# Four-tile weight rings, two sets of element loads, and 1 KB for dynamic DMAs' descriptors, in a two-layer RWKV-7 and S5 trunk

## The chip, the cores and the metric

The kernel runs on one core of one Trainium2 chip. The core has a matrix engine (TensorE, PE in the profile; its weight loads are listed as PEld), a vector engine (DVE), a scalar engine (ACT), GpSimd (POOL) and a sync engine (SP) that here issues nearly all transfers. Every engine works through its own list of instructions in the order in which the program holds them, and an instruction that waits holds up all that stand behind it on that engine. The metric is the device time of one execution in microseconds (us), as a median of several runs.

## The reference, cut to what matters

A sequence of 1024 frames with 1024 channels, in float32, goes through two layers. Layer 0 mixes over time with RWKV-7 (a matrix-valued state per head), layer 1 with a diagonal state-space layer (S5) and a gated linear unit; each mixer is followed by a squared-ReLU MLP with 4096 hidden channels, and each of the four sub-layers ends in a LayerNorm of `alpha * x + f(x)`.

```python
r, k, v = xr @ wr, xk @ wk, xv @ wv            # xr, xk, ... : x mixed with the frame before
a = sigmoid(a0 + (xa @ a1) @ a2);  g = sigmoid(xg @ g1) @ g2
state = state * w_t + sa * b_t + v_t * k_t     # per head, frame after frame
...
h = layer_norm(DN_ALPHA * h + mix, ...)
h = layer_norm(DN_ALPHA * h + square(relu(h @ w1)) @ w2, ...)
```

## The kernel before, in words

**Number format and weights.** Each float32 product is made of three products of a narrower type: an operand is split into a rounded part (hi) and the rest (lo). A weight tile of 128 x 512 numbers (256 KB, 2 KB of each partition) goes through three rings of the pool `wp`: `wraw` holds it as loaded by SP (line 215; lines 322, 476, 1135 and 1182 use the same ring), ACT casts it to `whi` (line 191 in `split`, or 220, 224), and DVE subtracts to get `wlo` (line 192), or `wlo` is loaded as it was saved earlier (line 223). `whi` and `wlo` are then read by the matmuls of line 256. `wraw` has two tiles, `whi` and `wlo` three each. A ring's tile can be written again only when its last reader is done, so SP waits at line 215 for ACT and DVE, ACT at line 191 for PE.

**Stages.** `rwkv_proj(0)` and `rwkv_proj(1)` make the projections r, k, v, a, g and the decay for the two halves (512 frames each) and store them in DRAM (`s_r`, `s_k`, `s_v`, `s_a`, `s_g`, `s_sg`). `core` then runs eight units of 256 frames x 512 channels, four per half. For a unit, `elem(m)` runs twice (j = 0, 1; I call these its two halves): it loads `ldk`, `ldsg`, `lda`, `ldr` (line 589), scans the decay (line 622 on DVE, which overwrites `ldsg`), makes `E` (line 625, ACT), `kf` (631 ACT, 633 and 643 POOL), `kk` (607, 620) and from these `AR` (636, 637) and `KB` (641, 642). `amat` (line 672, 676), `invert` (708 to 742) and the serial `chain` (780 to 803) follow, then `gnorm`. `KB` has two tiles, and a unit's `KB` is released by `kbtrans` (line 686) of that unit, so the next unit's first `KB` waits for it. The four `ld` tensors have one tile each: a half's loads wait for the last readers of the half before. Of these, line 642 reads `ldsg` last.

`wo(0)`, LayerNorm 1 and the MLP of the first half start when units 0 to 3 are through; from there on the MLP's matmuls fill PE. The S5 tables and `s5`, `glu`, the second MLP (`blocks`, and `both`, which shares products between the two halves) follow. The last blocks run in two column halves with kept weights (`kept`: `wraw` loaded at line 1135, cast to the tile `kt1` by ACT at line 1139), and `last_norm` ends the program.

**What sets the order.** Instructions are put in order per engine when the program is built, from their priorities (`rank`; a smaller number goes first), their dependencies and the free tiles of the rings. The first half of `rwkv_proj(0)` has the smallest numbers, units have 3000 upwards, and the rest of the projections 100000. A change of a ring's depth therefore moves instructions on all engines, although the set of instructions stays what it was.

Of the kernel before, what the change touches and what calls it, by code (L numbers as in the profile page):

```python
# [8 lines left out]
F32 = mybir.dt.float32  # L9
# [12 lines left out]
KB2 = 2  # L22
# [34 lines left out]
RK = (6000, 3000, 1000, 2500, 2000, 7000, 2600)  # L57
PB = 3
STB = 3
EB = (1, 1, 1, 1, (), 1)  # L60
GNG = (0, 0)
XM0 = False
G1L = True
# [16 lines left out]
def trunk(ctx, tc, A):  # L80
    nc = tc.nc
# [1 line left out]

    cp = ctx.enter_context(tc.tile_pool(name="cp", bufs=1))
    dr = ctx.enter_context(tc.tile_pool(name="dr", bufs=1, space=DRAM))
    wp = ctx.enter_context(tc.tile_pool(name="wp", bufs=3))
    ap = ctx.enter_context(tc.tile_pool(name="ap", bufs=1))
    tp = ctx.enter_context(tc.tile_pool(name="tp", bufs=2))
    pd = ctx.enter_context(tc.tile_pool(name="pd", bufs=3, space=PSUM))
# [78 lines left out]
    def weave(op, share=1.0):  # L168

        if anchor[0] is not None or not woven:  # L170
            return
        due[0] += share
        anchor[0] = op
        while due[0] >= 1 and woven:
            due[0] -= 1
            with rank(woven[0][1]):
                if next(woven[0][0], None) is None:
                    woven.pop(0)
                else:
                    woven[0][1] = tc.cur_priority  # L180
        anchor[0] = None
# [8 lines left out]
    def split(src, hi, lo, e=None):  # L190
        S.copy(hi, src)  # L191
        op = (e or V).tensor_sub(lo, src, hi.bitcast(F32))  # L192
        if e is None or e is V:
            behind(op)
            weave(op, pace_[0])
# [8 lines left out]
    nw = [0]  # L204
# [3 lines left out]
    def wload(src, kt, n, key=None, halved=False):  # L208

        step = 512 // n  # L210
        out = []
        for k0 in range(0, kt, step):
            kept = low.get((key, k0)) if key else None
            raw = wp.tile([128, step, n], F32, tag="wraw", name="wraw", bufs=2)
            SP.dma_start(raw, src[:, k0 : k0 + step])
            hi = wp.tile([128, step, n], F32R, tag="whi", name="whi")
            lo = wp.tile([128, step, n], F32R, tag="wlo", name="wlo")
            nw[0] += 1
            if halved:
                S.mul(hi, raw, 0.5)  # L220
                weave(V.scalar_tensor_tensor(lo, raw, 0.5, hi.bitcast(F32), op0=ALU.mult, op1=ALU.subtract))
            elif kept is not None:
                SP.dma_start(lo.bitcast(F32).rearrange("p k n -> p (k n)"), kept)
                S.copy(hi, raw)
            else:
                split(raw, hi, lo, G if nw[0] % WLG[0] in WLG[1] and WLG[2] <= nw[0] < WLG[3] else V)
                if key and key[0] not in ("mw1", "mw2"):
                    low[key, k0] = dr.tile([128, 512], F32, name=f"low{len(low)}")
                    SP.dma_start(low[key, k0], lo.bitcast(F32).rearrange("p k n -> p (k n)"))
            out += [(hi[:, k], lo[:, k]) for k in range(step)]  # L230
        return out
# [23 lines left out]
    def mmb(p, w, x, **kw):  # L255
        bulk.append((PE.matmul(p, w, x, **kw).ins, x.shape[-1]))  # L256

    def mm3(p, whi, wlo, xh, xl, first, last):
        mmb(p, whi, xh, start=first, stop=False)
        mmb(p, whi, xl, start=False, stop=False)  # L260
        mmb(p, wlo, xh, start=False, stop=last)
# [37 lines left out]
    def psd():  # L299
        pool, tag = banks[0][nb[0] % len(banks[0])]  # L300
        nb[0] += 1
        return pool.tile([128, HT], F32, tag=tag, name="d")
# [13 lines left out]
    def rwkv_proj(H):  # L316
# [1 line left out]
        xs = []  # L318

        def wraw(nm, k0):  # L320
            w = wp.tile([128, 4, 128], F32, tag="wraw", name="wsc", bufs=2)
            SP.dma_start(w, A[nm][:, k0 : k0 + 4])
            return w

        first = []
        for k in range(KT):
            t = ap.tile([128, HT + 1], F32, tag="xs", name="xs", bufs=8)
# [123 lines left out]
        def store_out(out, n, e):  # L451
            (ST if out in STO else SP).dma_start(scr[out][n * 128 : (n + 1) * 128, t0 : t0 + HT], e)
# [19 lines left out]
        def gate(n):  # L472
            if n % 4 == 0:
                wg[0] = wload(A["g2a"][:, n // 4], 4, 128, f"g2a{n}")
                rawb = wp.tile([128, 512], F32, tag="wraw", name="w2raw", bufs=2)
                SP.dma_start(rawb, A["g2b"][:, n * 128 : n * 128 + 512])
                wg[1] = wp.tile([128, 512], F32R, tag="whi", name="w2st")
                S.copy(wg[1], rawb)
                V.tensor_sub(wg[1][64:128], rawb[64:128], wg[1][64:128].bitcast(F32))
            q = n % 4  # L480
            p = psd()
            mm3(p, wg[0][q][0], wg[0][q][1], gx[0], gx[1], True, False)
            mmb(p, wg[1][:, q * 128 : (q + 1) * 128], h2, start=False, stop=True)
            e = tp.tile([128, HT], F32, tag="ev", name="ev", bufs=EVB)
            S.copy(e, p)
            store_out("g", n, e)
# [41 lines left out]
        else:  # L528
            for n in range(KT):
                rates(n)  # L530
            for n in range(KT):
                gate(n)
# [11 lines left out]
        for cb in range(4):  # L544
            pp = [psd(), psd()]
            for k0 in range(0, KT, 2):
                w = wload(A["wv"][cb][:, k0 : k0 + 2], 2, 256, f"wv{cb}-{k0}")
                for kk in range(2):
                    k = k0 + kk
# [28 lines left out]
    def elem(m):  # L578
# [5 lines left out]
        for j in range(2):  # L584
            n0 = 4 * D.q + 2 * j
            ld = {}
            for nm in ("k", "sg", "a", "r"):
                t = kp.tile([128, 512], F32, tag="ld" + nm, name="ld" + nm, bufs=EB[3] if nm in EB[4] else 1)
                SP.dma_start(t.rearrange("p (i t) -> p i t", i=2),
# [13 lines left out]

            sq = kp.tile([128, HT], F32, tag="sq", name="sq", bufs=EB[0])
            kk = kp.tile([128, HT], F32, tag="kk", name="kk", bufs=EB[1])
            for i in range(2):
# [15 lines left out]
            V.tensor_tensor_scan(cs, cmask.rearrange("p c l -> p (c l)"), cs, 0.0, op0=ALU.mult, op1=ALU.add)  # L622
            E = kp.tile([128, 8, L + 1], F32, tag="E", name="E", bufs=EB[5])
            G.memset(E[:, :, 0:1], 1.0)
# [3 lines left out]

            kf = kp.tile([128, HT], F32, tag="kf", name="kf", bufs=EB[2])
            for i in range(2):  # L630
# [483 lines left out]
    def blocks(i, h, xo, qbuf):  # L1114

        nw = 512 // KB2
        qs = {}

        def up(b):
            qs[b] = []  # L1120
            pace_[0] = PACEU[i]
            for n in range(KB2):
                p = psd()
                dense(p, wload(A["mw1"][i, b * KB2 + n], KT, 128, ("mw1", i, b * KB2 + n)), xo)
                r = tp.tile([128, HT], F32, tag="ev", name="rl", bufs=EVB)
                S.activation(r, p, AF.Relu)  # L1126
                S.activation(r, r, AF.Square)
                qt = qbuf[:, n + KB2 * (b % 2)]
                split(r, qt[:, 0], qt[:, 1])
                qs[b].append((qt[:, 0], qt[:, 1]))  # L1130
            pace_[0] = 1.0

        def kept(src, part):
            raw = wp.tile([128, KB2, nw], F32, tag="wraw", name="wraw", bufs=2)
            SP.dma_start(raw, src)
            hi, lo = (jp.tile([128, HT], F32R, tag=t, name="k" + t, bufs=8).rearrange("p (k n) -> p k n", k=KB2)
                      for t in ("t1", "t2"))
            SP.dma_start(lo.bitcast(F32).rearrange("p k n -> p (k n)"), part)
            S.copy(hi, raw)
            return [(hi[:, k], lo[:, k]) for k in range(KB2)]  # L1140

        def down(b, first=False, cs=slice(0, HT), keep=None):
            for n2 in range(C // nw):
                if keep is None:
                    w = wload(A["mw2"][i, b, n2], KB2, nw, ("mw2", i, b, n2))
                else:
                    if (b, n2) not in keep:
                        keep[b, n2] = kept(A["mw2"][i, b, n2], low[("mw2", i, b, n2), 0])
                    w = keep[b, n2]
                for n in range(nw // 128):  # L1150
                    p = psd()[:, cs]
                    dense(p, [(x[:, n * 128 : (n + 1) * 128], y[:, n * 128 : (n + 1) * 128]) for x, y in w],
                          [(x[:, cs], y[:, cs]) for x, y in qs[b]])
                    z = h[n2 * (nw // 128) + n][:, cs]
                    if first:
                        weave(V.scalar_tensor_tensor(z, z, ALPHA, p, op0=ALU.mult, op1=ALU.add), PACED[i])
                    else:
                        weave(V.tensor_add(z, z, p), PACED[i])  # L1158

        return up, down  # L1160
# [12 lines left out]
    def both(i, hP, hQ, P, Q, tops, first):  # L1173

        nw = 512 // KB2
# [2 lines left out]
        qs = {}  # L1178

        def raw(pool, tag, f, k0):  # L1180
            t = pool.tile([128, 4, 128], F32, tag=tag, name="raw", bufs=2)
            SP.dma_start(t, A["mw1"][i, f][:, k0 : k0 + 4])
            return t

# [477 lines left out]
    with rank(99100):  # L1662
        for k in range(4):
            a = t1[k]
# [107 lines left out]
```

## Time and profile before

| | before |
|---|---|
| median of 3 runs | 2596.31 us (2596.01 to 2599.6) |
| the profiled execution's own time | 2585.47 us |
| its span | 2583.5 us |
| mean granted PE clock | 0.975 of full speed |
| ACT, DVE, POOL busy | 1210.5, 1794.0, 406.0 us |
| loads of `wraw`, all lines together | 256 KB each, median 2.7 to 4.2 us to landing |

A column of waits reads "who waited, for whom: us in total, times, longest". In the table of windows each stretch has the busy time of each engine, then the mean granted clock of PE (1.00 is full speed), the share of the DMA engines that was busy, and GB/s. The chain of work that ended last is given as start, length and what ran; a chain that passes through an instruction says that nothing earlier could have released what came after it.

### The profile page before, as it was taken

What the parts mean: (1) busy time and instruction counts of PE and PEld (TensorE: products, weight loads), DVE (VectorE), ACT (ScalarE), POOL (GpSimd) and SP (SyncE); (2) the same over time, 40 slices, a digit from 0 to 9 for tenths busy, and PEclk for the clock granted to TensorE, in tenths of its full rate; (3) what the DMA queues carried; (4) which work ended last, traced back from release to release, by engine and by line L of the source; (5) the groups of instructions that cost most, each with busy time, mean ns of one, the idle gap of its engine ahead of it and who ended that gap; (6) DMA issues with size and microseconds to landing.
All of it is one profiled execution on the core that took longest, in us unless ns stands there. A gap on an engine that the chain in (4) does not pass through costs nothing.

```text
span 2583.5 us, 43873 instructions
## 1 busy us (share of the span) xinstructions
PE 2466.0 (95%) x16684; PEld 2002.0 (77%) x16684; DVE 1794.0 (69%) x3443; ACT 1210.5 (47%) x2165; POOL 406.0 (16%) x336
## 2 busy tenths in 40 slices
PE   7989989989989999999999999999999999999997
PEld 5779767788767888777777878887887888888886
DVE  7477687577787776899886665676657555656555
ACT  7555575454454443345634444334565333343334
POOL 3110441331211102001000000100222111111111
PEclk9999989999899999999999999999999999999998
DMA  4765455664222324446565553244261111111233
GB/s 152 261 200 184 160 198 172 190 186 152 93 70 78 104 86 126 141 122 165 162 226 192 176 175 111 95 162 160 94 197 60 49 54 50 48 58 49 78 122 114
DMA packets 217682, 340.66 MB, mean 132 GB/s; under 512 B 21248, under 2 KB 81792, under 8 KB 217472
## 3 DMA queue, kind: packets, MB, share of 16 engines
q1 hardware_dynamic: 216320, 335.77, 40.9%
q8 instruction: 131, 2.15, 0.4%
q10 hardware_dynamic: 1152, 2.10, 0.2%
q14 instruction: 79, 0.65, 0.1%
HBM read 267.53 MB, written 70.25 MB: 131 GB/s over the span
## 4 chain that ended last, share of the span: by engine, by line
PE 69%; DVE 13%; DMA 9%; ACT 5%; issue 3%; SPq 1%; POOL 0%; ACTq 0%; DVEq 0%; POOLq 0%
PE d L256 51%; PE d L1195 10%; DVE wlo L192 2%; PE pA L672 1%; DMA wraw<-in_mw_dram 1%; ACT whi L191 1%; DMA yl<-s_y 1%; DVE hA L1158 1%; DMA pre<-in_mw_dram 1%; DMA ldsg<-s_sg 1%; DMA s_y<-yg 1%; PE pR L780 1%; DMA lda<-s_a 1%; DVE oAl L192 1%; PE pq L934 1%
## 5 line engine op out<-in xcount | busy, mean ns | idle before, releaser
L191 ACT CAST whi<-wraw 128x512 fp32r<-128x512 f32 x424 | 261.6, 619 | 487.1 <-PE d L256 249.8
L192 DVE TENSOR_TENSOR wlo<-wraw,whi 128x512 fp32r<-128x512 f32 x424 | 317.4, 750 | 201.1 <-ACT whi L191 197.2
L256 PE MATMUL d<-qbuf,whi 128*128 128x512 f32 x1152 | 365.2, 399 | 9.8 <-ACT rl L1126 4.7
L256 PE MATMUL d<-oAh,whi 128*128 128x512 f32 (+1 forms) x752 | 303.2, 409 | 13.1 <-ACT ev L493 5.5
L256 PE MATMUL d<-oAl,whi 128*128 128x512 f32 (+1 forms) x752 | 302.1, 403 | 7.7 <-DVE oAl L942 4.4
L256 PE MATMUL d<-oAh,wlo 128*128 128x512 f32 (+1 forms) x752 | 301.2, 404 | 3.5 <-DMA wlo<-low 1.9
L256 PEld LDWEIGHTS d<-qbuf,whi 128*128 128x128 f32 x1152 | 212.2, 189 | 63.1 <-DVE hA L1158 7.8
L256 PE MATMUL d<-qbuf,wlo 128*128 128x512 f32 x576 | 225.5, 394 | 0.0
L256 PE MATMUL d<-oBh,whi 128*128 128x512 f32 x496 | 195.9, 395 | 0.4 <-DVE hA L1158 0.4
L256 PE MATMUL d<-oBh,wlo 128*128 128x512 f32 x496 | 195.8, 395 | 0.0
L256 PE MATMUL d<-oBl,whi 128*128 128x512 f32 x496 | 193.7, 391 | 0.0
L256 PEld LDWEIGHTS d<-oAh,whi 128*128 128x128 f32 (+1 forms) x752 | 143.1, 192 | 48.0 <-ACT ev L493 7.8
L256 PEld LDWEIGHTS d<-oAl,whi 128*128 128x128 f32 (+1 forms) x752 | 144.4, 193 | 38.7 <-DVE oAl L942 4.8
L256 PEld LDWEIGHTS d<-oAh,wlo 128*128 128x128 f32 (+1 forms) x752 | 144.3, 193 | 36.2 <-DVE wlo L192 2.7
L256 PE MATMUL d<-ql,whi 128*128 128x512 f32 x416 | 163.1, 392 | 0.0
L256 PE MATMUL d<-qh,whi 128*128 128x512 f32 x416 | 162.0, 389 | 0.0
L256 PE MATMUL d<-qh,wlo 128*128 128x512 f32 x416 | 158.0, 394 | 0.0
L256 PEld LDWEIGHTS d<-qbuf,wlo 128*128 128x128 f32 x576 | 108.9, 189 | 24.4 <-issue 0.5
L1158 DVE TENSOR_TENSOR hA<-hA,d 128x512 f32<-128x512 f32 x136 | 92.0, 683 | 28.8 <-PE d L256 27.7
L1158 DVE TENSOR_TENSOR hB<-hB,d 128x512 f32<-128x512 f32 (+1 forms) x160 | 97.6, 631 | 20.1 <-PE d L256 18.9
L256 PEld LDWEIGHTS d<-oBh,wlo 128*128 128x128 f32 x496 | 93.2, 188 | 21.9 <-issue 0.8
L256 PEld LDWEIGHTS d<-oBh,whi 128*128 128x128 f32 x496 | 93.3, 188 | 21.5 <-issue 2.0
(495 smaller groups left out, 5268.6 us busy)
## 6 DMA issues: line engine op xcount, KB each, us to landing
wraw<-in_mw_dram SPq DMA_DIRECT2D x356, 256.0 KB, 2.7
wlo<-low SPq DMA_DIRECT2D x92, 256.0 KB, 2.9
wraw<-in_glu_dram SPq DMA_DIRECT2D x64, 256.0 KB, 2.7
low<-wlo SPq DMA_DIRECT2D x52, 256.0 KB, 2.6
raw<-in_mw_dram SPq DMA_DIRECT2D x52, 256.0 KB, 2.7
wraw<-in_wk_dram SPq DMA_DIRECT2D x32, 256.0 KB, 3.2
wraw<-in_wr_dram SPq DMA_DIRECT2D x32, 256.0 KB, 3.7
wraw<-in_wv_dram SPq DMA_DIRECT2D x32, 256.0 KB, 4.2
```

Source lines behind the costliest of these rows:

```text
L191: S.copy(hi, src)
L192: op = (e or V).tensor_sub(lo, src, hi.bitcast(F32))
L256: bulk.append((PE.matmul(p, w, x, **kw).ins, x.shape[-1]))
L672: prods.append(PE.matmul(pp[h][:, cc, i], D.KB[j][hs, u].rearrange("p j l -> p (j l)"), D.AR[j][hs, u].rearrange("p j l -> p (j l)"), star ...
L780: hop.append(PE.matmul(pR[hs, i], at[:, h, c, i, 0], vsa[:, cl, h, i], start=True, stop=True))
L934: PE.matmul(pq[:, j : j + 1], q[:, j * 128 : (j + 1) * 128], ones_c[:, 0:1], start=k + j == 0, stop=k == KT - 1, skip_group_check=True)
L1158: weave(V.tensor_add(z, z, p), PACED[i])
L1195: PE.matmul(p, w[:, k], x, start=not add and k + j == 0, stop=k == 3 and j == 2, skip_group_check=True)
```

## The change

`wraw` gets four tiles at all places that use the ring (line 1181, which takes either pool, only for `wp`), and `whi` and `wlo`, which take the pool's default, four instead of three. The four `ld` tensors get two tiles each. To make room, the space that the program sets aside in each partition for descriptors of dynamic DMAs is set to 1 KB. No instruction is added or removed on any engine.

```diff
-EB = (1, 1, 1, 1, (), 1)
+EB = (1, 1, 1, 2, ("k", "sg", "a", "r"), 1)
...
-    wp = ctx.enter_context(tc.tile_pool(name="wp", bufs=3))
+    wp = ctx.enter_context(tc.tile_pool(name="wp", bufs=4))
...
-            raw = wp.tile([128, step, n], F32, tag="wraw", name="wraw", bufs=2)
+            raw = wp.tile([128, step, n], F32, tag="wraw", name="wraw", bufs=4)
...
-            w = wp.tile([128, 4, 128], F32, tag="wraw", name="wsc", bufs=2)
+            w = wp.tile([128, 4, 128], F32, tag="wraw", name="wsc", bufs=4)
...
-                rawb = wp.tile([128, 512], F32, tag="wraw", name="w2raw", bufs=2)
+                rawb = wp.tile([128, 512], F32, tag="wraw", name="w2raw", bufs=4)
...
-            raw = wp.tile([128, KB2, nw], F32, tag="wraw", name="wraw", bufs=2)
+            raw = wp.tile([128, KB2, nw], F32, tag="wraw", name="wraw", bufs=4)
...
-            t = pool.tile([128, 4, 128], F32, tag=tag, name="raw", bufs=2)
+            t = pool.tile([128, 4, 128], F32, tag=tag, name="raw", bufs=4 if pool is wp else 2)
...
-    nc = bacc.Bacc("TRN2", target_bir_lowering=False, num_devices=1)
+    nc = bacc.Bacc("TRN2", target_bir_lowering=False, num_devices=1, dynamic_dma_scratch_size=1024)
```

The places where the order changes, and on which the prediction rests, are three. The first is DVE in unit 2, at the step from its first half to its second. `KB_3091` is the first half's, `KB_3157`, `ldsg_3120` and `AR_3156` are the second half's; `hd` and `oAl` belong to the projections of the second 512 frames. Before:

```order
L641 TENSOR_TENSOR KB_3091<-kf_3086,ldsg_3054 64x8x64
L642 SCALAR_TENSOR_TENSOR KB_3091<-lda_3056,ldsg_3054 64x8x64
L403 TENSOR_TENSOR hd_4551<-d_4471,e2_4549 128x511
L408 TENSOR_TENSOR hd_4551<-d_4471,carry_p_135 128x1
L192 TENSOR_TENSOR oAl_4465<-hd_4460,oAh_4464 128x512
L622 SCALAR_TENSOR_TENSOR ldsg_3120<-cmask_111,ldsg_3120 128x512
L192 TENSOR_TENSOR oAl_4467<-hd_4551,oAh_4466 128x512
L626 COPY PL_3051<-E_3147 128x2x4
L636 TENSOR_TENSOR AR_3156<-ldr_3124,E_3147 128x8x64
L650 COPY bo_3050<-pb_3100 128x2x4
L613 TENSOR_SCALAR rn_3136<-pss_3131 128x8
```

Now the second half's scan, its copy to `PL` and its first `AR` are gone from this place:

```order
L641 TENSOR_TENSOR KB_3091<-kf_3086,ldsg_3054 64x8x64
L642 SCALAR_TENSOR_TENSOR KB_3091<-lda_3056,ldsg_3054 64x8x64
L827 TENSOR_REDUCE vr_3302<-osq_3300 128x8
L828 TENSOR_SCALAR vr_3302<-vr_3302 128x8
L650 COPY bo_3050<-pb_3100 128x2x4
L844 SCALAR_TENSOR_TENSOR o_2728<-o_2728,vr_3302,lg_2846 128x64 x8
L622 SCALAR_TENSOR_TENSOR ldsg_3708<-cmask_111,ldsg_3708 128x512
L613 TENSOR_SCALAR rn_3136<-pss_3131 128x8
```

The scan that stands here now is unit 3's (`ldsg_3708`); that of unit 2's second half went far ahead, to where unit 0 is still being inverted (`x1_1139`, `xh_1140`):

```order
L676 TENSOR_TENSOR AT2_2676<-pA_2678,amask_122 128x2x256
L676 TENSOR_TENSOR AT2_2676<-pA_2677,amask_122 128x2x256
L718 TENSOR_TENSOR xh_1140<-xh_1140,x1_1139 128x19x6
L622 SCALAR_TENSOR_TENSOR ldsg_3120<-cmask_111,ldsg_3120 128x512
L192 TENSOR_TENSOR wlo_2005<-wraw_2002,whi_2004 128x512
L716 TENSOR_TENSOR x1_1139<-xa_1138,xh_1140 128x126
```

The second place is PE in the first projections, where `pss_970`, the first matmuls of unit 0, stands among the bulk matmuls `d`. Before, it stood ahead of the r projection's first tile (`d_779`):

```order
L256 MATMUL d_735<-oAh_247,whi_746 128x512
L256 MATMUL d_735<-oAl_248,whi_746 128x512
L256 MATMUL d_735<-oAh_247,wlo_747 128x512
L611 MATMUL pss_970<-hsel_103,sq_965 128x2 x4
L256 MATMUL d_779<-oS_483,whi_782 128x512 x2
L256 MATMUL d_779<-oS_483,wlo_783 128x512
```

Now it stands behind the four r tiles of the first group (`d_779` to `d_911`, 24 matmuls each) and ahead of `d_1296`:

```order
L256 MATMUL d_911<-oS_489,whi_922 128x512
L256 MATMUL d_911<-oS_490,whi_922 128x512
L256 MATMUL d_911<-oS_489,wlo_923 128x512
L611 MATMUL pss_970<-hsel_103,sq_965 128x2 x4
L256 MATMUL d_1296<-stash_336,whi_1290 128x512
L256 MATMUL d_1297<-stash_336,whi_1290 128x512
```

The third place is ACT at the end, in the last blocks. `kt1` are the kept weights' casts, each waiting for a load of `wraw`; `rl` is the ReLU that empties a block's PSUM tile `d`, and `rb` and `hA` belong to the LayerNorm of the first half. Before, casts and the others alternate:

```order
L1139 CAST kt1_25072<-wraw_25070 128x512
L1127 ACTIVATE rl_24979<-rl_24979 128x512
L1139 CAST kt1_25094<-wraw_25092 128x512
L191 CAST qbuf_24452<-rl_24979 128x512
L1139 CAST kt1_25116<-wraw_25114 128x512
L1020 ACTIVATE hA_7562<-hA_7562,pv_89 128x512
L1020 ACTIVATE hA_7602<-hA_7602,pv_89 128x512
L1139 CAST kt1_25138<-wraw_25136 128x512
```

Now all eight casts stand ahead of the first `rl`:

```order
L1139 CAST kt1_25094<-wraw_25092 128x512
L1139 CAST kt1_25116<-wraw_25114 128x512
L1139 CAST kt1_25138<-wraw_25136 128x512
L1139 CAST kt1_25160<-wraw_25158 128x512
L1139 CAST kt1_25182<-wraw_25180 128x512
L954 COPY rb_24739<-rs_24736 128x512
L1126 ACTIVATE rl_24979<-d_24942 128x512
L1127 ACTIVATE rl_24979<-rl_24979 128x512
L191 CAST qbuf_24452<-rl_24979 128x512
```

So the last `rl` no longer has a cast, and thus a load, between itself and the first one.

## The prediction

> **What bounds the kernel now.** I begin with the page's list of engines and its chain of work that ended last.
>
> ```profile
> PE 2466.0 (95%) x16684; PEld 2002.0 (77%) x16684; DVE 1794.0 (69%) x3443; ACT 1210.5 (47%) x2165; POOL 406.0 (16%) x336
> ...
> PE 69%; DVE 13%; DMA 9%; ACT 5%; issue 3%; SPq 1%; POOL 0%; ACTq 0%; DVEq 0%; POOLq 0%
> ```
>
> PE is busy for 95% of the span, so at most 2583.5 - 2466.0 = 117.5 us of waiting can go, plus what PE loses to a lowered clock. Yet only 69% of the chain runs over PE: in some places work on DVE, transfers and ACT ends last. The busy times by stretch say where.
>
> ```profile
> core 0: us, PE busy (x) PEld busy (x) DVE busy (x) ACT busy (x) POOL busy (x), PEclk, DMA share, GB/s
> 0.00:140.00 140.00, 119.50 (x567) 88.59 (x568) 83.66 (x146) 88.14 (x153) 34.23 (x40) 0.97 0.61 205
> 140.00:700.00 560.00, 513.56 (x5179) 425.74 (x5179) 416.40 (x971) 309.23 (x582) 148.51 (x129) 0.94 0.54 171
> 700.00:1010.00 310.00, 300.54 (x2398) 241.69 (x2399) 233.75 (x505) 142.45 (x259) 43.58 (x34) 0.97 0.29 88
> 1010.00:1950.00 940.00, 915.47 (x5763) 736.32 (x5761) 689.42 (x1235) 432.52 (x760) 79.88 (x56) 1.00 0.49 154
> 1950.00:2520.00 570.00, 569.66 (x2480) 466.93 (x2481) 335.44 (x497) 210.94 (x359) 92.66 (x67) 1.00 0.20 64
> 2520.00:2584.00 64.00, 47.26 (x304) 42.73 (x302) 35.37 (x94) 27.26 (x54) 7.19 (x10) 0.85 0.34 113
> ```
>
> From 1950 to 2520 us PE waits 0.3 us; nothing can be won there. The units before the first MLP (140 to 700) leave PE 560.0 - 513.6 = 46.4 us idle at a mean clock of 0.94, which is another 0.06 x 560 = 34 us. The start leaves 20.5 us idle, the tail 16.7, the stretch from 1010 to 1950 24.5. Next I ask whom PE waited for, from 140 to 700.
>
> ```profile
> PE d L256 <- ACT oAh L191: 9.2, 3, 4.1
> ...
> PE d L256 <- ACT whi L224: 2.6, 3, 1.7
> ...
> PE d L256 <- DMA wlo<-low: 1.9, 1, 1.9
> ...
> PE d L256 <- DVE wlo L192: 1.4, 2, 1.2
> ```
>
> Direct waits for a weight tile are 2.6 + 1.9 + 1.4 = 5.9 us. Deeper weight rings therefore have little to give on PE itself; what binds is the serial path of the units.
>
> **The change part by part.** No instruction is added, so every cost is one of place and time. The sum is made on the profiled execution (span 2583.5, its own time 2585.5); the median shown, 2596.3, is 10.8 us above it, and I carry the difference in us over unchanged.
>
> *Two sets of element loads.* These are the waits of DVE and ACT from 140 to 700, then the chain through unit 2.
>
> ```profile
> DVE ldsg L622 <- DMA ldsg<-s_sg: 20.4, 9, 5.8
> ...
> ACT kf L631 <- DMA lda<-s_a: 8.5, 5, 4.3
> ```
>
> ```profile
> 304.37 0.62 DVE KB L642
> 305.00 3.02 DMA ldsg<-s_sg
> ...
> 308.11 1.24 DVE ldsg L622
> ...
> 321.86 0.69 DVE kk L620
> ```
>
> The first half's last `KB` ends at 304.99 and releases the one `ldsg`; the load starts at 305.00, and DVE stands before the scan of line 622 until it lands at 308.0. With a second tile the load needs no release, and the new order has this scan some hundred microseconds earlier, in unit 0's inversion. The 3.0 us of load and 1.2 of scan leave the place. What is late next is the normalisation of `kk`: `pss`, `rn` and `pn` go through PE and POOL, and `kk` comes at 321.86, long after `kf` could be ready. So the second half of the unit gains less than 4.2 us: the scan delayed `rn` behind it on DVE, and only that part is on the path. All nine waits are 20.4 us, with ACT's 8.5 at most 28.9. The gain lies between 0 (each hidden behind `kk`) and 28.9 (all on the path to the first MLP). I take half of DVE's, **-10 us**, since the chain passes through the scan but its successor is near.
>
> *Weight rings, 140 to 1950.* The 5.9 us of direct waits can go; below, another wait may end at the same time. I take -4, with 0 and -6 as ends. From 700 to 2520 the matrix engine's waits name weights with 0.3 us in all, in this row of the stretch from 1010 to 1950:
>
> ```profile
> PE d L256 <- DVE wlo L192: 0.3, 1, 0.3
> ```
>
> So I cost the rings at 0 there: PE, 97% busy or more, is the cover.
>
> *Weight rings at the start.* Here `wraw` is loaded, scaled on POOL and split. SP's own waits up to 60 us, and the chain:
>
> ```profile
> SPq L322 <- DVE wlo L192: 23.4, 8, 6.6
> ```
>
> ```profile
> 19.04 0.61 DVE wlo L192
> ...
> 19.66 2.74 DMA wsc<-in_g1a_dram
> ```
>
> With two tiles the load at 19.66 starts when DVE is done; with four it has long landed. DVE is nearly full there, so of 2.7 us on the chain, and others like it that are shorter, I take **-3**, between 0 and -6.
>
> *Unit 0 begins later.* Better fed, the first projections, which outrank the units, keep PE, and `pss_970` stands behind four r tiles more: 96 matmuls. A later unit 0 costs only if the units and not PE then end last. Nothing is lost if the work passed over would have to be done anyway (0); by the order the first `pA` of unit 0 comes 9 us of matmuls later (+9). I take **+4**.
>
> *The tail.* The chain, and PE's timeline:
>
> ```profile
> 2531.57 4.63 DMA wraw<-in_mw_dram
> ...
> 2536.22 0.63 ACT kt L1139
> ...
> 2538.87 0.58 ACT rl L1126
> ```
>
> ```profile
> 2533.02 4.27 PE L256 MATMUL d<-qbuf,kt 128*128 128x256 f32 x36
> 2539.50 11.47 PE L256 MATMUL d<-qbuf,kt 128*128 128x256 f32 x84 [2.21 <-ACT rl L1126]
> ```
>
> The `rl` on which PE waits is held up on ACT by casts `kt` that wait for `wraw`, four loads one behind the other. With four tiles they overlap, and in the new order all casts stand ahead and are done while PE still works on the block before. At the pace of the 36 matmuls (4.27 / 36 = 0.119 us) the 84 take 10.0 instead of 11.5 us; with the wait of 2.21 this is 3.7. I take **-4**, from 0 to -5.
>
> *The 1 KB.* It costs nothing by the queues that carry the program's own transfers:
>
> ```profile
> q1 hardware_dynamic: 216320, 335.77, 40.9%
> ...
> q10 hardware_dynamic: 1152, 2.10, 0.2%
> ```
>
> They are SP's and ACT's; POOL issues none. I take 0 and bound it by 0 above, for lack of any user.
>
> Sum: -10 - 4 - 3 + 4 - 4 = **-17**: execution 2585.5 - 17 = 2568.5, median 2596.3 - 17 = **2579**.
>
> *A rule on the clock.* Two stretches show half speed:
>
> ```profile
> 72.90:76.30 3.40, 2.94 (x7) 2.37 (x8) 2.02 (x3) 3.21 (x6) 0.00 (x0) 0.50 0.96 332
> ...
> 2540.80:2544.20 3.40, 3.40 (x19) 3.40 (x18) 1.09 (x3) 2.83 (x5) 0.00 (x0) 0.50 0.87 331
> ```
>
> The second follows PE's wait of 2.21 us, so even that wait brought 3.4 us at 0.50, and the 1.5 us that I count for slow matmuls in the tail include it. The Trainium skill ("TensorE: Matmul & The Clock Gate", Part 1: The HAM clock gate) has the clock halved after at least one idle window of about 3.4 us. By that rule a wait of 2.2 us costs no clock and the tail would gain 2 us instead of 4; the row speaks against it, and the sum follows the row.
>
> **The rivals.**
>
> *Nothing measurable.* `kk` ends each second half whatever `kf` and the scan do (321.86 above), so the loads give 0. Left are -4 - 3 + 4 - 4 = -7 at best, and with the weights' waits replaced by others -3: median 2589 to 2593. For it: PE's longest waits in the units are for `oAh` (9.2), which the change does not touch. Against: the chain itself runs through the load.
>
> *Slower: the weights crowd out the units.* One more cast, subtraction and transfer of weights can stand ahead of a unit's step in each in-order queue.
>
> ```profile
> L191 ACT CAST whi<-wraw 128x512 fp32r<-128x512 f32 x424 | 261.6, 619 | 487.1 <-PE d L256 249.8
> L192 DVE TENSOR_TENSOR wlo<-wraw,whi 128x512 fp32r<-128x512 f32 x424 | 317.4, 750 | 201.1 <-ACT whi L191 197.2
> ...
> wraw<-in_mw_dram SPq DMA_DIRECT2D x356, 256.0 KB, 2.7
> ...
> wraw<-in_wv_dram SPq DMA_DIRECT2D x32, 256.0 KB, 4.2
> ```
>
> The price per half of a unit is 0.62 + 0.75 + (4.2 - 2.7) = 2.9 us; eight halves lie before the first MLP: +23. With the rest of the sum (-7) and no gain from the loads this is +16, median 2612. It decides once a unit's loads land later than now by more than they start earlier, some 2 us. Against it: units outrank all but the first projections. The Trainium skill ("DMA: Bandwidth & Descriptors", Queues, rings and completion order) says that each of the 16 engines takes up one queue's descriptors in ring order, so a unit's load would stand behind weights already queued; the landing of 4.2 us in the busy v projection agrees in direction.
>
> *Much faster.* All loads on the path, all bounds at their best: -29 - 6 - 6 - 5 = -46, median 2550.
>
> *The change doesn't do what it says.* The rings might go unused, or the small set-aside might hold transfers up. SP's waits for the ring at the start, 23.4 us, say that it is wanted, and no transfer uses the set-aside; I give this no chance of its own.
>
> **How the numbers follow.** About 0.2% (5 us) is what a measurement of this kernel can tell from no change. My forecast, between -5 and -42, gets 0.58; much faster 0.06; nothing measurable 0.19, part of which (-3) is within 5 us and part (-7) just outside, balanced by weaker forms of the forecast; slower 0.17, half of it milder than +16, since the order on every engine is new and small collisions add to that mechanism. Faster 0.64, same 0.19, slower 0.17. The range leaves out about 0.08 on either side: 2554 to 2606.
>
> **What would show it.** Right: DVE's waits for `ldsg` from 140 to 700 fall from 20.4 us to a few, units 2 and 3 come earlier, LayerNorm 1 (PE's `pq` at 695) some 10 to 17 us earlier, and the wait for `rl` near the end is gone. From there to 2520 the times only shift. Wrong: the waits for `ldsg` go but `KB` of the second halves keeps its distance to that of the first; the units' loads land later than now; or PE waits longer for casts of ACT, where weights now stand ahead.

## The result, and the profile after

The changed kernel takes **2565.17 us** (median of 6 runs, 2561.68 to 2575.26), the kernel before, beside it, 2596.11 us (6 runs, 2592.58 to 2599.6). The ratio is **0.9894, interval 0.9873 to 0.9914**: 0.0106 x 2596 = 27.5 us faster, with 22 to 33 as ends. (The two medians lie 30.9 us apart; I go by the ratio, to which the interval belongs.) Forecast were 17, in a range that reaches to 42.

The profiled execution after took 2565.43 us (span 2563.6), close to its median; that of before, 2585.47, was 10.6 us below its own. Between the two profiles only 20 of the 27 us are therefore to be seen.

The page of the kernel after, its engines and its chain of work that ended last:

```profile
PE 2470.6 (96%) x16684; PEld 2012.9 (79%) x16684; DVE 1784.2 (70%) x3443; ACT 1213.8 (47%) x2165; POOL 409.6 (16%) x336
...
PE 79%; DVE 10%; DMA 5%; ACT 4%; issue 2%; POOL 0%; SPq 0%; ACTq 0%; DVEq 0%; POOLq 0%
```

The work is the same, but the chain now runs over PE for 79% instead of 69%; transfers fell from 9% to 5%. The busy times by stretch, columns as before:

```profile
0.00:140.00 140.00, 122.64 (x573) 92.50 (x574) 84.31 (x146) 91.00 (x161) 36.01 (x40) 0.96 0.68 228
140.00:700.00 560.00, 529.62 (x5233) 439.98 (x5232) 420.07 (x990) 311.75 (x584) 155.92 (x132) 0.92 0.54 171
700.00:1010.00 310.00, 297.93 (x2372) 238.85 (x2372) 231.92 (x510) 142.01 (x256) 46.61 (x37) 0.98 0.30 93
1010.00:1950.00 940.00, 921.04 (x5785) 746.05 (x5786) 693.81 (x1228) 435.82 (x764) 73.95 (x51) 0.99 0.48 151
1950.00:2520.00 570.00, 569.82 (x2498) 467.52 (x2497) 324.60 (x486) 216.71 (x366) 90.98 (x67) 1.00 0.22 67
```

From 140 to 700 us PE is idle for 560.0 - 529.6 = 30.4 us, where it was 46.4. Part of that is taken back by the clock, whose mean there is 0.92 instead of 0.94 (0.02 x 560 = 11 us at most). From 1950 to 2520 nothing has changed. PE's waits from 140 to 700 us:

```profile
PE pq L934 <- DVE hA L993: 5.2, 1, 5.2
PE pU L790 <- ACT vsa L787: 4.6, 3, 2.7
PE d L256 <- DVE oAl L192: 3.8, 6, 1.7
PE d L256 <- ACT oAh L191: 3.5, 3, 2.2
...
PE d L256 <- ACT whi L224: 2.1, 1, 2.1
```

The wait for `oAh`, the operand of the projections, fell from 9.2 us to 3.5, although the prediction said that the change does not touch it. And the wait whose end should have carried the gain is still there; DVE's list for the same stretch has

```profile
DVE ldsg L622 <- DMA ldsg<-s_sg: 23.6, 11, 4.8
```

against 20.4 before. The tail did what was said: the 120 matmuls with `kt`, which were 36, a wait of 2.21 us and 84, now run through in 14.30 us instead of 4.27 + 2.21 + 11.47 = 17.95.

```profile
2518.50 14.30 PE L256 MATMUL d<-qbuf,kt 128*128 128x256 f32 x120
```

So the forecast holds some six tenths of the gain, and one of its reasons is in doubt: which part of the change carries it?

### The profile page after: what moved, and what is told of

Read it like the earlier page. It is cut to its first block, busy times and chain, and to the rows that moved or that the text cites. A ratio compares the mean times of both kernels' runs of the same rounds, so it can differ in the third digit from the quotient of the medians.

```text
span 2563.6 us, 43894 instructions
## 1 busy us (share of the span) xinstructions
PE 2470.6 (96%) x16684; PEld 2012.9 (79%) x16684; DVE 1784.2 (70%) x3443; ACT 1213.8 (47%) x2165; POOL 409.6 (16%) x336
## 4 chain that ended last, share of the span: by engine, by line
PE 79%; DVE 10%; DMA 5%; ACT 4%; issue 2%; POOL 0%; SPq 0%; ACTq 0%; DVEq 0%; POOLq 0%
PE d L256 59%; PE d L1195 9%; PE pA L672 1%; PE pR L780 1%; DVE wlo L192 1%; DVE oAl L192 1%; PE pX L785 1%; PE pk L1427 1%; DVE xh L718 1%; DVE x L716 1%; PE pU L790 1%; PE pq L934 1%; PE pb L648 1%; PE pO L801 1%; PE pO L799 1%
## 5 line engine op out<-in xcount | busy, mean ns | idle before, releaser
L192 DVE TENSOR_TENSOR wlo<-wraw,whi 128x512 fp32r<-128x512 f32 x424 | 308.6, 730 | 198.6 <-ACT whi L191 187.4
L256 PEld LDWEIGHTS d<-oAh,wlo 128*128 128x128 f32 (+1 forms) x752 | 143.8, 192 | 30.9 <-issue 1.0
L256 PEld LDWEIGHTS d<-qbuf,wlo 128*128 128x128 f32 x576 | 109.2, 190 | 23.5
L1158 DVE TENSOR_TENSOR hB<-hB,d 128x512 f32<-128x512 f32 (+1 forms) x160 | 98.0, 630 | 26.3 <-PE d L256 25.3
```

## The experiments

Two theories came first. A: the second set of loads carries most, as the prediction has it. B: the rings do. A third question came up on the way: a change of tiles also changes the order of instructions on every engine, so what is the tiles' doing and what the order's? All ratios are against the kernel before, run on the same chip in the same turns; 0.001 is 2.6 us.

### The parts, each with the order that its own build gives

A copy of before shows what no change looks like.

> The kernel before, once more, with a profile on the same chip as the runs below. The change measured -31 us by medians (2596.1 to 2565.2), but only -20 us by the two profiled executions (2585.5 to 2565.4). If the profile of before happened to be a fast execution, this one's execution time lies at 2592 to 2600 and its extra time is spread over the program. If the two profiles tell the true difference, it lies at 2583 to 2588 again, and the medians carry something that the profiles do not show.

Measured: 0.9992 (0.9975 to 1.0009), 2583.92 us. Its profile's span, 2583.3, is 0.2 from that of before. That is the expectation's second case: median and profiled execution (2585.22) agree here, and it is the medians of the first measurement that lie 10 us higher.

The set-aside alone:

```diff
-    nc = bacc.Bacc("TRN2", target_bir_lowering=False, num_devices=1)
+    nc = bacc.Bacc("TRN2", target_bir_lowering=False, num_devices=1, dynamic_dma_scratch_size=1024)
```

> Only the 1 KB for dynamic DMAs' descriptors; all rings as before, and the order of every engine as before. My step: 0 (ratio 0.999 to 1.001). If the set-aside were used by this program's transfers, they would be held up: slower by 5 us or more, with longer landing times.

Measured: 1.0003 (0.9987 to 1.002). It costs nothing. All kernels that follow have it too. This one has the same order as before on every engine, so its profile is another one of the program before: its span is 2579.2 us. Three profiles of one order thus lie 4.3 us apart, and differences of single profiles below that say nothing.

The rings alone (every line of the change that sets `bufs`, but not `EB`):

```diff
-    wp = ctx.enter_context(tc.tile_pool(name="wp", bufs=3))
+    wp = ctx.enter_context(tc.tile_pool(name="wp", bufs=4))
...
-            raw = wp.tile([128, step, n], F32, tag="wraw", name="wraw", bufs=2)
+            raw = wp.tile([128, step, n], F32, tag="wraw", name="wraw", bufs=4)
```

> Only the weight rings (wraw, whi, wlo of four tiles) and the 1 KB; the element loads keep one set. Theory A (mine): the rings give -4 in the units, -3 at the start, -4 in the tail and cost +4 by unit 0's later start, so about -7 us against before, ratio 0.997, and DVE's waits for ldsg stay near 20 us from 140 to 700. Rival B (the rings carry the change): -20 to -31 us, ratio 0.988 to 0.992. Rival C (only the order as a whole counts, the parts do not add): anything, with both parts together differing from their sum by over 10 us.

The loads alone:

```diff
-EB = (1, 1, 1, 1, (), 1)
+EB = (1, 1, 1, 2, ("k", "sg", "a", "r"), 1)
```

> Only the two sets of element loads and the 1 KB; the weight rings stay as before. Theory A: -10 to -24 us, ratio 0.991 to 0.996, unit 0 starts as early as before, LayerNorm 1 (PE pq) 10 us or more before 695, DVE's waits for ldsg from 140 to 700 far below 20 us; the tail keeps its wait of PE for rl. Rival B: 0 to -5 us, since kk ends each half anyway.

Measured: the rings 0.9909 (0.9888 to 0.993), some 24 us faster; the loads 1.002 (1.0007 to 1.0033), some 5 us slower. The rings lie in the range of rival B, the loads in no range that was given. Theory A falls in this form: alone, with the order they get, the loads lose. Against the copy's trace their units 2 and 3 begin their chains (line 780) 23.5 and 24.2 us earlier, as hoped, but unit 4 only 6.5, and LayerNorm 1 comes 14.4 us later. In their build other waits have grown on DVE, for ACT's copies in the inversion and for the loads of r. From the kernel with the loads alone, DVE's waits from 140 to 700 us:

```profile
DVE xa L708 <- ACT x L707: 19.0, 5, 10.2
DVE ldsg L622 <- DMA ldsg<-s_sg: 16.0, 9, 3.2
...
DVE AR L636 <- DMA ldr<-s_r: 11.4, 5, 3.9
```

In the copy the first was 7.4 us. Whether more tiles or another order did this can't be told from such a pair.

### The same order, only the tiles differ

So the order was held. The program is built twice: first with the tiles of the kernel whose order is wanted, then with other tiles and with edges from each instruction to the next on its engine, SP's transfers included. The edges fix the order and add no wait.

```diff
+    order = order_of(*build())
+    EB, WR, WS = (1, 1, 1, 2, ("k", "sg", "a", "r"), 1), 4, 4
+    nc, _ = build(order)
...
+                for n in order:
+                    i = byname[n]
+                    if i.engine in last:
+                        tc.add_manual_dep(i, last[i.engine], why, reason="kept order")
+                    last[i.engine] = n
```

`WR` is the number of tiles of `wraw`, `WS` that of `whi` and of `wlo`. First all tiles of the change in the order of before; and beside it, without a held order, each ring by itself.

> All buffers of the change (four-tile rings, two sets of loads, 1 KB), but every engine, SP's transfers too, keeps the order of before: the order is taken from a build with before's rings and fixed by edges that only order and add no wait. So only the waits for a free tile are different from before. Theory W (fewer waits for free tiles carry the 24 us that the rings gave alone): ratio 0.989 to 0.993, 18 to 28 us faster than before. Theory O (the rings carry it by the order that the program gets when it is built with them, which puts bulk matmuls where PE stood idle from 100 to 400 us): ratio 0.997 to 1.000, at most 8 us faster, and PE's idle time from 100 to 400 us stays near the 28.9 us of the copy of before.

> Only wraw gets four tiles (and 1 KB); whi and wlo keep three, loads one set. Its order on PE is almost that of the four-tile rings together. Theory R1 (the tile as loaded is the ring that matters: SP may issue a weight load while two others still wait for ACT and DVE): ratio 0.990 to 0.993 like the rings together (0.9909). Theory R2 (the split tiles matter: ACT's casts may run one tile further ahead of PE): 0.998 to 1.000.

> Only whi and wlo get four tiles (and 1 KB); wraw keeps two, loads one set. Theory R1: ratio 0.998 to 1.001, no gain. Theory R2: 0.990 to 0.993, the gain of the rings together. If order by chance is worth several us, it may fall anywhere between 0.995 and 1.004, and the two parts will not add up to the rings' -24 us.

Measured: **f1_order_before 0.9899 (0.988 to 0.9917)**, f2_wraw 0.9999 (0.9984 to 1.0014), f3_split 1.0051 (1.0032 to 1.0071). Theory O falls: with not one instruction moved, the tiles bring 26 us, as much as the whole change does with its own order. The other two bear out neither R1 nor R2: f2_wraw lies where R2 has it, but f3_split, for which R2 has a gain, lies above every range. Each ring alone, in its own order, brings nothing or loses 13 us.

Then the parts, each in the order of before:

```diff
+    EB, WR, WS = (1, 1, 1, 2, ("k", "sg", "a", "r"), 1), 2, 3   # g1_loads_kept
+    EB, WR, WS = (1, 1, 1, 1, (), 1), 4, 4                      # g2_rings_kept
+    EB, WR, WS = (1, 1, 1, 1, (), 1), 4, 3                      # g3_wraw_kept
```

> Only the second set of element loads (and 1 KB), the rings as before, and the order of before on every engine. Theory L (in a fixed order the loads do carry part of it: the gap of 4.3 us on PE at 534 us, whose chain runs through a wait of ACT for lda, was 0.6 us in f1_order_before): ratio 0.996 to 0.998, 5 to 10 us faster, with that gap gone. Theory N (the rings alone carry it; the gap goes because weights come earlier): 0.999 to 1.001 and the gap stays.

> Only the four-tile rings (and 1 KB), loads with one set, and the order of before on every engine. Theory N: ratio 0.989 to 0.991, all of f1_order_before's gain (0.9899). Theory L: 0.992 to 0.995, the loads' part is missing. If the parts add up in a fixed order, this gain and that of g1_loads_kept together make f1_order_before's 24.6 us.

> Only wraw with four tiles (and 1 KB), whi and wlo with three, loads with one set, and the order of before on every engine. If wraw by itself takes waits away that lie on the path: ratio 0.992 to 0.996, and f2_wraw's 0.9999 was an order that gave it back. If SP stays held by the loads of wlo (line 223, which wait for PE: 70.4 us from 140 to 700 us in the copy of before, 21.7 in f1_order_before), so that the deeper wraw can't run ahead: 0.998 to 1.001, and that wait of SP stays near 70 us.

Measured, with the numbers from above (us worked out as ratio less 1, times 2586):

| tiles | in the order of before | us | in their own order | us |
|---|---|---|---|---|
| loads | 0.9977 (0.9965 to 0.9989) | -6 | 1.002 (1.0007 to 1.0033) | +5 |
| `wraw` | 0.996 (0.9946 to 0.9974) | -10 | 0.9999 (0.9984 to 1.0014) | 0 |
| all rings | 0.9956 (0.9937 to 0.9974) | -11 | 0.9909 (0.9888 to 0.993) | -24 |
| rings and loads | 0.9899 (0.988 to 0.9917) | -26 | 0.9894 (0.9873 to 0.9914) | -27 |

Three things follow. In a held order each part that was tried gains, and the loads do carry some of it: theory L rather than N, although the rings' 0.9956 lies just above the range that L gave. Of the rings it is `wraw` that gains; `whi` and `wlo` add nothing that can be measured. And the order that a build happens to give moves the time by -12 to +11 us in these rows, as much as the tiles themselves, while for the change as a whole it comes to nothing.

The two parts sum to 17 us and give 26 together. The 9 us between stand against some 7 or 8 that the three intervals leave open (an estimate: the root of the sum of their squares, 3.1, 4.7 and 4.8 us), so that the parts help each other is likely, and not settled by the times alone.

One wait that the expectation of g3_wraw_kept took for a cause is no measure of the gain. SP waited from 140 to 700 us at line 223 for a free tile of `wlo`; in the copy of before, in g3_wraw_kept and in g2_rings_kept:

```profile
SPq L223 <- PE d L256: 70.4, 29, 11.8
```

```profile
SPq L223 <- PE d L256: 78.7, 31, 8.7
```

```profile
SPq L223 <- PE d L256: 16.9, 11, 4.5
```

With `wraw` alone it even grew, and the kernel was 10 us faster; with all rings it was nearly gone, and that brought nothing more. Most of what SP waits there is, it seems, time by which it is ahead.

### The place where it shows

With a held order one instruction can be followed through the kernels. The longest wait of PE in the units is one for `oAh`. In the timelines of PE it stands so in the copy of before, with the loads, with the rings, and with both:

```profile
539.96 0.52 PE L256 MATMUL d<-whi,oAh 128*128 128x256 f32 x1 [4.11 <-ACT oAh L191]
```

```profile
531.58 0.39 PE L256 MATMUL d<-whi,oAh 128*128 128x256 f32 x1 [1.89 <-ACT oAh L191]
```

```profile
528.56 0.39 PE L256 MATMUL d<-whi,oAh 128*128 128x256 f32 x1 [0.95 <-ACT oAh L191]
```

```profile
522.85 0.39 PE L256 MATMUL d<-whi,oAh 128*128 128x256 f32 x1 [0.36 <-ACT oAh L191]
```

Why do a unit's loads and weight tiles shorten a wait for a projection's operand? ACT's timeline of the copy, ahead of that place:

```profile
528.74 0.60 ACT L631 ACTIVATE kf<-lda,kam,kah 128x256 f32<-128x256 f32 x1 [4.21 <-DMA lda<-s_a]
...
531.42 0.62 ACT L224 CAST whi<-wraw 128x512 fp32r<-128x512 f32 x1
531.94 0.58 ACT L506 COPY ev<-d 128x512 f32<-128x512 f32 x1
...
538.68 0.72 ACT L358 ACTIVATE m<-xs,pv 128x512 f32<-128x512 f32 x1 [3.36 <-DMA s_r<-ev]
539.31 1.12 ACT L191 CAST oAh<-m 128x512 fp32r<-128x512 f32 x2
```

ACT stood 4.21 us before `kf`, until `lda` had landed. Behind it in ACT's order stood casts of weights and evictions of PE's results, and behind the store of an eviction (`s_r<-ev`) the step that makes the next operand. PE is the last in that row, and no wait that PE shows here names a load or a weight tile. The same `kf` with the loads, with the rings and with both:

```profile
522.55 0.60 ACT L631 ACTIVATE kf<-lda,kam,kah 128x256 f32<-128x256 f32 x1 [5.43 <-DMA lda<-s_a]
```

```profile
520.49 0.60 ACT L631 ACTIVATE kf<-lda,kam,kah 128x256 f32<-128x256 f32 x1 [4.37 <-DMA lda<-s_a]
```

```profile
514.28 0.60 ACT L631 ACTIVATE kf<-lda,kam,kah 128x256 f32<-128x256 f32 x1 [1.74 <-DMA lda<-s_a]
```

Neither part alone takes ACT's wait away; both together take 2.5 us of it. The reason is on SP, which issues the load. With two sets of loads alone it gets to `lda` late, having stood 6.3 us before another load of line 589, whose data a store had not yet written, and 1.0 at line 223 for a free `wlo`; with the rings alone it stood 5.0 us before the load of `ldsg`, which it issues just ahead of `lda`, for a tile that the last `KB` releases. SP's waits in the 10 to 11 us before, loads first, then rings:

```profile
SPq L589 <- DMA s_r<-ev: 6.3, 1, 6.3
SPq L223 <- PE d L256: 1.0, 1, 1.0
```

```profile
SPq L589 <- DVE KB L642: 5.0, 1, 5.0
```

| | `lda` issued (SP's timeline) | ahead of `kf` | ACT's wait before `kf` | from `kf` to the cast `oAh` | PE's wait for `oAh` |
|---|---|---|---|---|---|
| copy of before | 524.80 | 3.94 us | 4.21 | 10.57 | 4.11 |
| loads | 517.03 | 5.52 | 5.43 | 8.37 | 1.89 |
| rings | 516.39 | 4.10 | 4.37 | 7.42 | 0.95 |
| both | 507.02 | 7.26 | 1.74 | 7.91 | 0.36 |

With both, the load is issued 7.26 us ahead of its reader instead of 3.9 to 5.5. At this wait the parts need each other: a second tile is of use only when SP is free to fill it. PE's wait for `oAh`, however, falls with each part alone, by 2.2 and 3.2 us, while ACT's wait before `kf` does not. What each part takes off by itself lies behind `kf`, where evictions and their stores come sooner.

Two limits of this place. The waits are the same in the two other profiles of the order of before (4.27 and 4.22 us on ACT, 4.13 and 4.07 on PE), but the times are not: `kf` begins there at 522.53 and 523.27 us, not at 528.74. Measured from these two, `kf` comes at most 0.7 us earlier with the loads, 2.0 to 2.8 with the rings and 8.3 to 9.0 with both; measured from the copy it is 6.2, 8.3 and 14.5, and the parts just add. So whether they help each other in time can't be read here. And with `wraw` alone (g3_wraw_kept), 10 us faster as a whole, ACT still waits 4.17 us and PE 3.68: the gain of that part is not made at this place.

### Further than the change

Last, the order of the kernel with rings alone, which was the fastest part, with more tiles in it: once with the second set of loads, once with rings of five.

```diff
+    EB, WR, WS = (1, 1, 1, 2, ("k", "sg", "a", "r"), 1), 4, 4   # f4_order_rings
+    EB, WR, WS = (1, 1, 1, 1, (), 1), 5, 5                      # g4_deeper
```

> All buffers of the change, with the order on every engine of the kernel with four-tile rings alone (fixed as in f1_order_before). So the second set of loads can only take waits away: the same order with more tiles. If the waits for ldsg (31.1 us from 140 to 700 us in the kernel with the rings alone) lie on the path at all, it is faster than that kernel by some us: ratio 0.986 to 0.990. If they are hidden, it is the same: 0.990 to 0.992.

> The order of the kernel with four-tile rings alone, on every engine, with wraw, whi and wlo five tiles deep and one set of loads: 6 of the 8 KB of the loads' second set go into the rings instead. Against four tiles in nearly the same order (0.9909) and four tiles with two sets of loads in the same order (0.9882). If four tiles are enough: 0.990 to 0.992. If ring waits still lie on the path: 0.986 to 0.989, better than with the loads.

Measured: 0.9882 (0.9862 to 0.9901), 2558.92 us, and 0.9877 (0.9856 to 0.9898), 2552.26 us. Both lie where more tiles were expected to help on, but their intervals overlap those of the rings alone (0.9909) and of the change (0.9894). That either beats the change is not shown.

## Why the prediction was right, step by step

The direction held, and the size was 10 us short. Where that lies is read from the kernels with a held order: the start of LayerNorm 1 (the first matmul of line 934), that of the last blocks (line 1195) and the end of the span, us in each profile. The first two come from rows like these, of the loads and of both parts, listed by the source line:

```profile
L1195 PE MATMUL d<-oBh,whi x104: 388/388/628, 1944.3 to 2430.4; 128*128 128x512 f32 x104
```

```profile
L1195 PE MATMUL d<-oBh,whi x104: 388/388/632, 1925.7 to 2411.6; 128*128 128x512 f32 x104
```

| stretch | three profiles in the order of before | loads | `wraw` | rings | both | after |
|---|---|---|---|---|---|---|
| to LayerNorm 1 | 695.5, 701.0, 693.2 | 692.9 | 693.3 | 691.7 | 684.7 | 686.6 |
| from there to the last blocks | 1249.6, 1245.9, 1250.1 | 1251.4 | 1242.5 | 1242.3 | 1241.0 | 1245.5 |
| from there to the end | 638.4, 636.4, 635.9 | 636.2 | 636.6 | 635.0 | 632.7 | 631.5 |

- **Loads, -10.** Right in kind, too large alone: -6. On top of the rings the loads are worth more: 0.9956 and 0.9899 in the order of before are 15 us apart, 0.9909 and 0.9882 in the order of the rings 7. "DVE's waits for `ldsg` from 140 to 700 fall from 20.4 us to a few" was wrong. They fell to 16.1 us with the loads in the held order, and in the changed kernel they are 23.6. What fell lay elsewhere, on ACT before `kf`: 8.5 us before, and no wait for `lda` from 140 to 700 us in the changed kernel (with the same tiles in the order of before it is still 6.7). The sum had counted that wait only in its upper bound.
- **Weight rings, 140 to 1950, -4, and 0 from 700 on.** This is the step that failed: "So I cost the rings at 0 there: PE, 97% busy or more, is the cover." In the second row of the table the four profiles with two `wraw` tiles lie between 1245.9 and 1251.4 (mean 1249.2), the three with four tiles between 1241.0 and 1242.5 (mean 1241.9): about **7 us** come from where nothing was booked. A share of 97% leaves 3% of 1250, some 37 us, and a wait named for another engine can still begin at a weight tile. Some 4 of the 7 us are idle time of PE (29.2 us in the mean of the four profiles, 25.3 in that of the three). Which single wait holds them stays open: in this stretch they are many, and each is short. The order counts here as well: the changed kernel, with its own, has 1245.5, only 3 us below the mean of the three profiles of before, and the rings with theirs (e1_rings) have 1228.5.
- **Weight rings at the start, -3.** Not seen. The first `pA` of unit 0 (line 672) starts at 128.7, 132.3 and 130.3 us in the three profiles before, and at 129.6 with the rings in the same order.
- **Unit 0 begins later, +4.** It did: its chain starts at 230.2 us instead of 218.9. But unit 2's starts 13 us and LayerNorm 1 9 us earlier than in the profile of before, and the order as a whole is worth nothing that can be measured (0.9894 with it, 0.9899 with the old one). One place was taken out of thousands that moved. No loss of 4 us is to be seen.
- **Tail, -4.** Right in kind: the wait for `rl` is gone, and 17.95 less 14.30 is 3.65 us on PE. But the size goes by one profile. In the copy and in e3_scratch the same matmuls with their wait took 16.04 and 15.23 us, without the slow stretch that the forecast counted, so the place is worth 0.9 to 3.7 us. Nor does it need the new order of the casts: with `wraw` alone in the order of before the 120 matmuls run through too, in 13.79 us. The third row falls by 6.9 in the profiles before and after (by 4.4 to 4.9 from the other two of before).
- **The 1 KB.** Costs nothing, as said: 1.0003.
- **The rival "weights crowd out the units".** Loads of `wraw` for the v projection took longer to land, 4.9 us at the median instead of 4.2, and the units' own loads, whose later landing the prediction named as a sign of being wrong, did land later: `ldsg` 4.5 us at the median instead of 3.1, `lda` 4.4 instead of 3.6. The gain came nonetheless. The Trainium skill's page "DMA: Bandwidth & Descriptors" (Queues, rings and completion order) describes the queue in which this could happen; here it did not outweigh the gain. "Nothing measurable" rested on PE's waits for `oAh`, "which the change does not touch"; the timelines above show that it does, at one such wait.

So the -17 was a sum with errors both ways: 3 too much at the start and 4 too much on the loads alone, against 7 from 700 us on and the 4 of unit 0 that were not lost. That makes -21, by sizes from a held order and from single profiles; that errors of opposite sign kept the sum near the result is luck. The rest, some 6 us, is of the size by which both parts together exceed their sum, which the prediction added up as if each stood alone. At `kf` the traces show one wait where they don't; that such waits make up the 6 us is not shown.

## What to carry to other kernels

Ask of a buffer not only who waits for it by name, but which in-order engine it stops, and what stands behind: here ACT, which makes an operand for which PE waits, stood before a unit's load, and that load was late because SP was held elsewhere, with either part alone. Where a build orders instructions by itself, hold the order before parts are compared: in their own orders the parts of this change read +5, 0 and +13, and in a held order each of those that was tried so gains. A busy share of 97% over 1250 us is not a cover, it is up to 37 us of waits that may have any cause.

## What the runs showed of the hardware

- The clock: the wait of 2.21 us before the last 84 matmuls was followed by a stretch of 3.4 us at 0.50 (in the prediction). In the copy of before the same wait was 1.53 us, and the stretch that follows has 1.00, so that the 84 took 10.24 instead of 11.47 us:

```profile
2540.72 10.24 PE L256 MATMUL d<-qbuf,kt 128*128 128x256 f32 x84 [1.53 <-ACT rl L1126]
```

```profile
2541.40:2544.80 3.40, 3.40 (x30) 3.21 (x28) 0.84 (x2) 3.40 (x6) 0.00 (x0) 1.00 1.03 387
```

  In e3_scratch and g1_loads_kept the wait was 0.70 and 1.10 us and the 84 took 10.26 us. So only the longest of four such waits was followed by half speed, at a cost of 1.2 us; that its length decided it is not shown. The Trainium skill ("TensorE: Matmul & The Clock Gate", Part 1: The HAM clock gate) asks for an idle window of about 3.4 us; the row of before does not agree with it, since PE's wait there was shorter, 2.21 us.
- The kernel before took 2596 us in the first measurement and 2585 to 2586 in the three turns of experiments (medians of 29, 17 and 22 runs, which spread from 2575 to 2598). A difference in us between kernels of different turns can be off by 10; the ratios within a turn can't in this way.
